# Batched q·kᵀ in float32: another order of the 32 KB chunks in the 4 MB loads

## The chip, the cores and the metric

The kernel runs on one core of one Trainium2 chip. The metric is the device time of one execution in microseconds. One execution was also taken with the hardware profiler, and all lines called "the profile" or "the trace" are from that one. The engines are called PE (matrix multiply), PEld (its weight loads), ACT, DVE and POOL (elementwise work) and SP (here it only issues transfers). SBUF is the on-chip memory of 128 partitions, PSUM is where PE writes, and sixteen DMA engines move data between SBUF and HBM.

## The reference

```python
def setup_inputs():
    batch, n_heads, seq, head_dim = 8, 12, 1024, 64
    # q, k: float32 [8, 12, 1024, 64], random, times 0.1

def reference(q, k):
    return np.einsum('bhid,bhjd->bhij', q, k).astype(np.float32)
```

That is 96 independent heads. Each multiplies a 1024 x 64 matrix by the transpose of another one, with no scaling and no softmax. The inputs are 50.3 MB, the output is 402.7 MB.

## The kernel before, in words

**Blocks of heads.** The 96 heads are taken in order in nine blocks of 2, 2, 4, 8, 16, 16, 16, 16 and 16 heads (numbers 0 to 8). `EARLY = 3` is the number of the 8-head block, so the 16-head blocks are those with `i > EARLY`: blocks 4 to 8. While a block is multiplied, the next one is loaded, cast and transposed.

**Loading (`Block.load`, line 171).** A 16-head block of q, and then one of k, is 16 x 1024 rows of 64 floats, 4 MB, contiguous in HBM. It goes into `x_sb`, 128 partitions of 32 KB, in one transfer: partition p takes the p-th chunk of 32 KB, that is 128 rows, so that a head lies in eight neighbouring partitions. `x_sb` holds one such load at a time, so a load waits until POOL has cast the one before. The ten loads of blocks 4 to 8 are issued from ACT's queue, q and k of a block in turn: one in block 2 (head 1), two in each of blocks 3 (heads 2 and 7), 4 (heads 4 and 10), 5 and 6 (heads 2 and 9), and the last, k of block 8, in block 7 (`LOADS` and the default beside it). So q of a block is loaded up to two blocks ahead and k in the block before. Blocks 0 to 3 are loaded from SP's and ACT's queues at the very start.

**Casting (`cast_quads`, line 220, POOL).** A load is cast to float16 in pieces called halves. Each piece is one of two parts (`part`) and one of two cuts (`c`) of the load, and is written by four POOL instructions of 32 partitions, which also rearrange the quadrants: afterwards a 32-partition quadrant holds 32 of the 64 columns of the head dimension for 32 chunks. Three buffers (`half_sb`) rotate.

**Transposing (`transpose_quads`, line 239, DVE).** One DVE instruction turns each 32 x 32 square of such a piece and writes into `qk_sb`. There the 64 values of the head dimension are in partitions, for half of the heads in partitions 0 to 63 and for the other half in 64 to 127, and the rows of a head are along the free axis. A piece has 128 x 2048 values. For a 16-head block there are eight pieces, four of q and four of k. In the output pattern the 32 chunks are the innermost dimension, with a step of R = 128 values of two bytes.

**Multiplying (`scores`, line 439, PE).** Head n of the block reads partitions `half * 64` onwards and column group g, with `half, g = divmod(n, N // 2)`: heads 0 to 7 from the lower partitions, 8 to 15 from the upper ones. A head takes eight weight loads and sixteen matmuls of 64 x 128 by 64 x 512. ACT copies each 128 x 2048 result from PSUM to one of three output buffers `o_sb` (line 297; in the first head DVE takes a part). The first matmul of a block waits for all eight transposes of that block (`self.ready`).

**Storing (line 310, SP).** Each head is stored in one transfer of 4 MB from its `o_sb`: partition p holds eight rows of the output, 32 KB. SP waits for the copies before it issues. ACT, in turn, waits for the store of three heads ago before it writes into that buffer.

**The tail (`scores_split`, lines 345 to 374).** The last head is stored in parts. One half of it goes out in an indirect transfer on POOL's queue, in which rows 16 to 19 and 48 to 51 (`APART = (16, 48)`) are left out. These rows are computed once more into a small buffer and stored by SP (line 433).

Of the kernel before, what the change touches and what calls it, by code (L numbers as in the profile page):

```python
# [9 lines left out]
P = 128  # L10
# [53 lines left out]
def kernel(  # L64
# [6 lines left out]
    nc = tc.nc  # L71
# [10 lines left out]
    PE_BLOCKS, EARLY = 2, 3  # L82
# [31 lines left out]
    class Ring:  # L114


        def __init__(self, bufs):
            self.bufs, self.n = bufs, 0
            self.busy = [[] for _ in bufs]
# [11 lines left out]
    n, at = S * D // P * 2, 8 * S // 2  # L131
# [15 lines left out]
    class Block:  # L147
        def __init__(self, i, first, N):
            self.i, self.first, self.N = i, first, N
            self.by_pe = i < PE_BLOCKS  # L150
            self.R = N * S // P
            self.elems = self.R * D
            self.cut = max(1, -(-self.R * 32 // CHUNK))
            self.raw = [None] * 2
            self.landed = [[] for _ in range(2)]
            self.rows = [None] * 2
            self.halves = {}
            self.qk = qk_sb[i % 2]
            self.ready = []
            self.over = []  # L160

        def load(self, x, eng, landing=None):
            events = []
            if self.raw[x] is None:
                at = x * self.elems if self.i == EARLY else 0
                self.raw[x] = x_sb[:, at : at + self.elems]
                landing = input_landing[x]
                events = list(input_busy)
            src = flat[x][self.first * S : (self.first + self.N) * S]
            eng.wait(events)  # L170
            dma = eng.eng.dma_start(
                out=self.raw[x], in_=src.rearrange("(p r) d -> p (r d)", p=P)
            )
            self.landed[x].append(landing.start(dma))

        def load_head(self, n, x, eng, landing):
# [54 lines left out]
        def transpose_quads(self, x, part, c, held=()):  # L231
            buf, cast, busy = self.halves.pop((x, part, c))
            n, m = self.N * S // 4, self.R // self.cut
            dst = self.qk[x][:, part * n : (part + 1) * n].rearrange(
                "c (i r) -> c r i", i=32
            )[:, c * m : (c + 1) * m]
            before = blocks[self.i - 2].over if self.i >= 2 else []
            done = dve.run(
                lambda: nc.vector.transpose(  # L239
                    out=dst, in_=buf.rearrange("p (r i) -> p r i", i=32)  # L240
                ),
                [cast, *held] + before,
            )
            busy.append(done)
            self.ready.append(done)
# [17 lines left out]
            self.ready.append(done)  # L263

        def scores(self, n, side, regions, w):
            half, g = divmod(n, self.N // 2)
            cs = slice(half * D, (half + 1) * D)
            qT = self.qk[0].rearrange("c (g m t) -> c g t m", t=NT, m=P)
            kT = self.qk[1].rearrange("c (g j) -> c g j", j=S)
            buf, out_free, out_busy = outs.next()  # L270
            written = {}
            for u in range(NT // w):
                ps, ps_free, ps_busy = regions.next()
                for tt in range(w):
                    stationary = qT[cs, g, w * u + tt]
                    done = pe.run(
                        lambda: load_weights(stationary, half * D),
                        self.ready if n == 0 and u == 0 else [],
                        signal=False,
                    )  # L280
                    for j in range(2):
                        at = tt * S + j * 512
                        done = pe.run(
                            lambda: multiply(
                                ps[:, at : at + 512],
                                stationary,
                                kT[cs, g, j * 512 : (j + 1) * 512],
                                half * D,
                            ),
                            ps_free,  # L290
                            signal=tt == w - 1 and j == 1,
                        )
                dst = buf[:, w * u : w * u + w].rearrange("p t j -> p (t j)")
                by_dve = w == 1 and u % 2
                copier = dve if by_dve else act
                copied = copier.run(
                    lambda: (nc.vector.tensor_copy if by_dve else nc.scalar.copy)(  # L297
                        out=dst, in_=ps[:, : w * S]
                    ),
                    out_free + [done],  # L300
                )
                written[copier] = copied
                ps_busy.append(copied)
                for do in side.get(u, []):
                    do()
            self.over = [done]
            sp.wait(written.values())
            if self.first + n == 0:
                sp.wait(blocks[EARLY].landed[0])
            dma = nc.sync.dma_start(  # L310
                out=of[self.first + n].rearrange("(p t) j -> p (t j)", p=P),
                in_=buf.rearrange("p t j -> p (t j)"),
            )
            out_busy.append(store_landing[id(buf)].start(dma))

        def scores_split(self, n, regions, w):
            half, g = divmod(n, self.N // 2)
            cs = slice(half * D, (half + 1) * D)
            qT = self.qk[0][cs, g * S : (g + 1) * S]
            kT = self.qk[1][cs, g * S : (g + 1) * S]  # L320
# [42 lines left out]
            for t in range(w):  # L363
                for c in range(2):
                    done = gps.run(
                        lambda: nc.gpsimd.tensor_copy(  # L366
                            out=packed[:, t, 0, :, c], in_=rows[:, t, :, c]
# [7 lines left out]
                    out=out.rearrange("b h (m t) j -> (b h m) (t j)", t=T),  # L375
                    out_offset=bass.IndirectOffsetOnAxis(ap=place_sb, axis=0),
                    in_=first,
# [9 lines left out]
            for c in range(4):  # L387
                row = 4 * APART[c // 2] + 8 * (c % 2)
                dst = head[row : row + 4 * w].rearrange("(e t) j -> e (t j)", t=w)
                self.store_part(sp, rest_landing, dst, rest[c:16:4])  # L390

            buf, out_free, _ = outs.next()
# [42 lines left out]
    def load_weights(stationary, at, to=0):  # L435
        return nc.tensor.ldweights(stationary, tile_position=(at, to))  # L436

    def multiply(dst, stationary, moving, at, to=0):
        return nc.tensor.add_instruction(  # L439
            mybir.InstMatmult(  # L440
                name=nc.get_next_instruction_name(),
                ins=[nc.tensor.lower_ap(moving), nc.tensor.lower_ap(stationary)],
                outs=[nc.tensor.lower_ap(dst)],
                start_tensor_calc=True,
                stop_tensor_calc=True,
                ldweights=False,
                tile_position=(at, to),
                tile_size=(D, stationary.shape[1]),
            )
        )  # L450
# [33 lines left out]
    for x in range(2):  # L484
# [7 lines left out]
                out=ident,  # L492
                in_=ident,
# [120 lines left out]
```

## Time and profile before

| | |
|---|---|
| median of 3 runs | 1060.29 us (1058.93 to 1060.81) |
| the profiled execution | 1059.37 us, of which its span 1057.6 us |
| granted clock of PE | 1.000 |
| HBM read, written | 50.33 MB, 402.78 MB |
| DMA, mean over the span | 429 GB/s |
| PE busy | 702.3 us (66%) |
| ACT busy | 695.4 us (66%) |
| DVE busy | 436.5 us (41%) |
| POOL busy | 357.8 us (34%) |

The span runs from the first to the last instruction. Busy shares are averages over the whole span; the profile also cuts the span into 40 slices of 26.4 us, where a digit is the busy share in tenths. For DMA that digit is the mean of the sixteen engines. Queue q1 is the one that SP issues on, q10 is ACT's, q0 is POOL's. In the list of groups an entry gives the line of the kernel, the engine, the operation, the tiles and shapes, the count, then the busy time and the mean of one in ns, then the idle time ahead of it and what ended most of that. In the list of transfers the last number is the median time from issue to landing. In the chain each line has the start, the length and the work.

### The profile page before, as it was taken

What the parts mean: (1) busy time and instruction counts of PE and PEld (TensorE: products, weight loads), DVE (VectorE), ACT (ScalarE), POOL (GpSimd) and SP (SyncE); (2) the same over time, 40 slices, a digit from 0 to 9 for tenths busy, and PEclk for the clock granted to TensorE, in tenths of its full rate; (3) what the DMA queues carried; (4) which work ended last, traced back from release to release, by engine and by line L of the source; (5) the groups of instructions that cost most, each with busy time, mean ns of one, the idle gap of its engine ahead of it and who ended that gap; (6) DMA issues with size and microseconds to landing.
All of it is one profiled execution on the core that took longest, in us unless ns stands there. A gap on an engine that the chain in (4) does not pass through costs nothing.

```text
span 1057.6 us, 3358 instructions
## 1 busy us (share of the span) xinstructions
PE 702.3 (66%) x1572; PEld 127.5 (12%) x802; DVE 436.5 (41%) x57; ACT 695.4 (66%) x385; POOL 357.8 (34%) x223
## 2 busy tenths in 40 slices
PE   6875744783756774765775675677477777777771
PEld 1111100110111110110111111111011111111110
DVE  2995929339254339137036706303930900000001
ACT  4766755674756765765875675577487777778771
POOL 7926455463708024605320830802290000000000
DMA  9999999999999999999999999999999999999998
GB/s 377 436 437 434 428 431 429 436 433 418 435 432 434 429 429 430 428 435 433 436 432 419 436 434 432 436 431 429 429 434 431 433 431 434 434 434 431 431 430 362
DMA packets 17185, 453.21 MB, mean 429 GB/s; under 512 B 1928, under 2 KB 1928, under 8 KB 2952
## 3 DMA queue, kind: packets, MB, share of 16 engines
q1 hardware_dynamic: 15008, 408.03, 89.6%
q10 hardware_dynamic: 2016, 42.99, 9.7%
q0 software_dynamic: 144, 1.97, 0.4%
q8 instruction: 9, 0.15, 0.0%
q14 instruction: 8, 0.07, 0.0%
HBM read 50.33 MB, written 402.78 MB: 428 GB/s over the span
## 4 chain that ended last, share of the span: by engine, by line
DMA 65%; ACT 15%; PE 8%; DVE 6%; POOL 4%; issue 1%; SPq 0%; ACTq 0%
DMA out_dram<-o_sb 60%; ACT o_sb L297 15%; PE ps_all L439 7%; DVE kT L239 4%; POOL half L220 3%; DMA x_sb<-in_k_dram 2%; DMA x_sb<-in_q_dram 2%; DVE qT L239 1%; DMA o_sb<-in_q_dram 0%; DVE x_sb L345 0%; DVE o_sb L345 0%; PE ps_all L253 0%; POOL qT L191 0%; DVE kT L260 0%; ACT kT L260 0%
## 5 line engine op out<-in xcount | busy, mean ns | idle before, releaser
L439 PE MATMUL ps_all<-kT,qT 64*128 64x512 f16 x1536 | 696.3, 617 | 325.5 <-ACT o_sb L297 307.7
L297 ACT COPY o_sb<-ps_all 128x2048 f32<-128x2048 f32 (+1 forms) x380 | 687.5, 1859 | 330.1 <-DMA out_dram<-o_sb 285.6
L220 POOL CAST half<-x_sb 32x2048 f16<-32x2048 f32 x176 | 332.1, 1887 | 431.3 <-DMA x_sb<-in_q_dram 176.2
L239 DVE STREAM_TRANSPOSE qT<-half 128x2048 f16<-128x2048 f16 x22 | 203.0, 9434 | 218.3 <-PE ps_all L439 117.8
L239 DVE STREAM_TRANSPOSE kT<-half 128x2048 f16<-128x2048 f16 x22 | 203.0, 9466 | 176.4 <-ACT o_sb L297 150.7
L436 PEld LDWEIGHTS <-qT 64*128 64x128 f16 x768 | 124.1, 162 | 894.5 <-issue 873.2
L345 DVE COPY x_sb<-ps_all 128x2048 f32<-128x2048 f32 x1 | 2.3, 2292 | 183.1 <-PE ps_all L439 183.1
L374 POOL DMA_INDIRECT out_dram<-x_sb,place x1 | 1.2, 1153 | 185.7 <-DVE x_sb L345 185.7
L366 POOL COPY rest_q<-qT 64x8 f16<-64x8 f16 x4 | 0.6, 196 | 51.1 <-DVE kT L239 51.1
L239 DVE STREAM_TRANSPOSE kT<-kT 128x1024 f16<-128x1024 f16 x2 | 9.4, 4893 | 0.0
L239 DVE STREAM_TRANSPOSE qT<-qT 128x1024 f16<-128x1024 f16 x2 | 9.2, 4786 | 0.0
L220 POOL CAST qT<-o_sb 32x1024 f16<-32x1024 f32 x8 | 8.3, 1034 | 1.2 <-DMA o_sb<-in_q_dram 0.8
L220 POOL CAST kT<-o_sb 32x1024 f16<-32x1024 f32 x8 | 8.3, 1034 | 0.5
L260 DVE COPY qT<-ps_all 128x1024 f16<-128x1024 f16 x2 | 2.4, 1224 | 11.2 <-PE ps_all L253 11.2
L297 DVE COPY o_sb<-ps_all 128x1024 f32<-128x1024 f32 x4 | 4.9, 1224 | 4.4 <-PE ps_all L439 4.4
L253 PE MATMUL ps_all<-ident,qT 128*128 128x128 f16 x16 | 2.1, 311 | 6.9 <-POOL qT L191 6.8
L345 ACT COPY x_sb<-ps_all 128x2048 f32<-128x2048 f32 (+1 forms) x2 | 3.7, 1860 | 2.1 <-PE ps_all L439 2.1
L260 ACT COPY kT<-ps_all 128x1024 f16<-128x1024 f16 x1 | 1.0, 1012 | 4.9 <-PE ps_all L253 4.9
L345 DVE COPY o_sb<-ps_all 128x2048 f32<-128x2048 f32 x1 | 2.3, 2291 | 3.7 <-PE ps_all L439 3.7
L191 POOL CAST qT<-o_sb 128x512 f16<-128x512 f32 x4 | 2.3, 613 | 3.9 <-DMA o_sb<-in_q_dram 3.9
L260 ACT ACT_TABLE_LOAD x1 | 1.3, 1283 | 2.8 <-issue 2.8
L260 DVE COPY kT<-ps_all 128x1024 f16<-128x1024 f16 x1 | 1.2, 1225 | 4.4 <-PE ps_all L253 4.4
(18 smaller groups left out, 14.5 us busy)
## 6 DMA issues: line engine op xcount, KB each, us to landing
out_dram<-o_sb SPq DMA_DIRECT2D x95, 4096.0 KB, 21.7
x_sb<-in_q_dram ACTq DMA_DIRECT2D x5, 4096.0 KB, 23.8
x_sb<-in_k_dram ACTq DMA_DIRECT2D x5, 4096.0 KB, 24.7
x_sb<-in_q_dram SPq DMA_DIRECT2D x1, 2048.0 KB, 14.6
x_sb<-in_k_dram SPq DMA_DIRECT2D x1, 2048.0 KB, 19.4
out_dram<-o_sb SPq DMA_DIRECT2D x1, 2048.0 KB, 17.9
o_sb<-in_k_dram ACTq DMA_DIRECT2D x4, 256.0 KB, 4.9
o_sb<-in_q_dram SPq DMA_DIRECT2D x4, 256.0 KB, 5.2
```

The source lines that it names most:

```text
L191: lambda: nc.gpsimd.tensor_copy(out=rows[:, :, h], in_=self.raw[x][:, h * n : (h + 1) * n].rearrange("p (r d) -> p r d", d=D),),
L220: lambda: nc.gpsimd.tensor_copy(out=dst[q0 : q0 + 32].rearrange("p (r d) -> p r d", d=32), in_=raw[32 * b : 32 * b + 32, c * m : (c + 1) * ...
L239: lambda: nc.vector.transpose(out=dst, in_=buf.rearrange("p (r i) -> p r i", i=32)),
L253: lambda: nc.tensor.transpose(t_ps[:, t], rows[:, t], ident),
L260: lambda: copy(out=dst, in_=t_ps.rearrange("c t m -> c m t")), [done]
L297: lambda: (nc.vector.tensor_copy if by_dve else nc.scalar.copy)(out=dst, in_=ps[:, : w * S]),
L345: lambda: (nc.vector.tensor_copy if copier is dve else nc.scalar.copy)(out=dst[:, t * S : (t + w) * S], in_=ps[:parts, : w * S]),
L366: lambda: nc.gpsimd.tensor_copy(out=packed[:, t, 0, :, c], in_=rows[:, t, :, c]),
L374: nc.gpsimd.indirect_dma_start(out=out.rearrange("b h (m t) j -> (b h m) (t j)", t=T), out_offset=bass.IndirectOffsetOnAxis(ap=place_sb, a ...
L436: return nc.tensor.ldweights(stationary, tile_position=(at, to))
L439: return nc.tensor.add_instruction(mybir.InstMatmult(name=nc.get_next_instruction_name(), ins=[nc.tensor.lower_ap(moving), nc.tensor.lower ...
```

## The change

In blocks 4 to 8, which the new flag `woven` marks, the chunk of a load that a partition takes is another one: partition 8e + j (e from 0 to 15, j from 0 to 7) takes chunk 16j + e, where it took chunk 8e + j. The source of the transfer has three dimensions for that, e, j and the 8192 floats of a chunk; the destination is written as before. Head n of the block has chunks 8n to 8n + 7. With the new order they are in partitions 8e + j with j = n // 2, and e from 0 to 7 for an even head or 8 to 15 for an odd one. After the casts, which are the same, the even heads are therefore in partitions 0 to 63 and the odd ones in 64 to 127, and each of the eight pieces holds a part of every head of a parity. The transposes write the 32 chunks in a four-dimensional pattern (rows, then e, then j innermost, with a step of 1024 values between neighbouring j), and a head reads `half, g = n % 2, n // 2`. The order in which heads are computed and stored, and the blocks 0 to 3, are the same.

```diff
@@ class Block, __init__
             self.by_pe = i < PE_BLOCKS
+            self.woven = i > EARLY
             self.R = N * S // P
...
+        def where(self, n):
+            return (n % 2, n // 2) if self.woven else divmod(n, self.N // 2)
+
         def load(self, x, eng, landing=None):
...
-            dma = eng.eng.dma_start(
-                out=self.raw[x], in_=src.rearrange("(p r) d -> p (r d)", p=P)
-            )
+            dst, src = self.raw[x], src.rearrange("(p r) d -> p (r d)", p=P)
+            if self.woven:
+                src = src.rearrange("(j e) f -> e j f", j=8)
+            dma = eng.eng.dma_start(out=dst, in_=src)
...
         def transpose_quads(self, x, part, c, held=()):
             buf, cast, busy = self.halves.pop((x, part, c))
             n, m = self.N * S // 4, self.R // self.cut
-            dst = self.qk[x][:, part * n : (part + 1) * n].rearrange(
-                "c (i r) -> c r i", i=32
-            )[:, c * m : (c + 1) * m]
+            src = buf.rearrange("p (r i) -> p r i", i=32)
+            if self.woven:
+                dst = self.qk[x].rearrange("c (j q e r) -> c q r e j", q=2, e=4, r=self.R)
+                dst = dst[:, part, c * m : (c + 1) * m]
+                src = src.rearrange("p r (e j) -> p r e j", e=4)
+            else:
+                dst = self.qk[x][:, part * n : (part + 1) * n].rearrange(
+                    "c (i r) -> c r i", i=32
+                )[:, c * m : (c + 1) * m]
...
-                lambda: nc.vector.transpose(
-                    out=dst, in_=buf.rearrange("p (r i) -> p r i", i=32)
-                ),
+                lambda: nc.vector.transpose(out=dst, in_=src),
...
         def scores(self, n, side, regions, w):
-            half, g = divmod(n, self.N // 2)
+            half, g = self.where(n)
...
         def scores_split(self, n, regions, w):
-            half, g = divmod(n, self.N // 2)
+            half, g = self.where(n)
```

## The prediction

> **What bounds the kernel now.** I read the rows of forty slices first, then the table of queues, then the chain that ended last, then the waits, and only then the groups of instructions.
>
> ```profile
> DMA  9999999999999999999999999999999999999998
> GB/s 377 436 437 434 428 431 429 436 433 418 435 432 434 429 429 430 428 435 433 436 432 419 436 434 432 436 431 429 429 434 431 433 431 434 434 434 431 431 430 362
> DMA packets 17185, 453.21 MB, mean 429 GB/s; under 512 B 1928, under 2 KB 1928, under 8 KB 2952
> ...
> q1 hardware_dynamic: 15008, 408.03, 89.6%
> q10 hardware_dynamic: 2016, 42.99, 9.7%
> ...
> DMA 65%; ACT 15%; PE 8%; DVE 6%; POOL 4%; issue 1%; SPq 0%; ACTq 0%
> ```
>
> The sixteen DMA engines are busy in every slice; no compute engine is above 66%. q1 is SP's queue (the stores), q10 is ACT's (the loads of the 16-head blocks). Two prices follow. Stores: 89.6% of 1057.6 us is 947.6 us on each engine for 408.03/16 = 25.50 MB, so 32 KB take 1.218 us. Loads: 9.7% is 102.6 us for 42.99/16 = 2.687 MB, so 32 KB take 1.251 us. The single packet records of the trace say where that difference sits: nearly all packets of 32 KB take 1.213 us, but in four of the five loads of k 22 to 30 of the 128 take longer, up to 2.33 us.
>
> ```profile
> PE ps_all L439 <- ACT o_sb L297: 307.7, 185, 11.6
> ACT o_sb L297 <- DMA out_dram<-o_sb: 285.6, 86, 11.6
> ```
> ```profile
> 151.19 36.71 DVE kT L239 x4
> 187.90 0.05 issue
> 187.94 1.94 PE ps_all L439 x4
> ...
> 197.38 21.36 DMA out_dram<-o_sb
> ```
>
> The first fence is from the list of waits (total us, times, longest): PE waits for ACT, and ACT for stores to free an output buffer, so the compute side runs ahead of the DMA. The second is the chain in order of time at the start of block 4, the tightest place: four transposes hold PE until 187.94, yet the store issued at 197.38 lands 21.36 us later. A store alone fills the engines for 9.7 us (8 packets of 1.218 us each), so 11.7 us of earlier work was still queued. Compute may be 11.7 us late there before the DMA runs dry; in the stretches with stores alone the same margin is 12.0 us (21.7 less 9.7). The time is therefore the DMA engines' work, the slowest engine's, plus a start and a tail. The execution took 1059.37 us, 1.8 more than its span, and 0.9 under the median of the runs, 1060.29.
>
> **The change part by part.** Bytes, loads, queues, issue points, head order and waits stay. Three things move.
>
> (1) The addresses on PE's side: head n reads half n%2, group n//2. Same shapes and counts, 1536 matmuls of 617 ns, and PE idles 325.5 us before them: nothing.
>
> (2) The writes of 40 of the 44 large transposes (eight for each of blocks 4 to 8).
>
> ```profile
> L239 DVE STREAM_TRANSPOSE kT<-half 128x2048 f16<-128x2048 f16 x22 | 203.0, 9466 | 176.4 <-ACT o_sb L297 150.7
> ...
> L239 DVE STREAM_TRANSPOSE kT<-kT 128x1024 f16<-128x1024 f16 x2 | 9.4, 4893 | 0.0
> ```
>
> Neighbouring results now lie 2048 bytes apart in runs of 8, where they lay 256 bytes apart. The rows hold three steps already: 64 bytes (block 2), 128 (block 3) and 256. They cost 4893/1024 = 4.78 and 9466/2048 = 4.62 ns a column, so the step does not set the price. I take zero. Against it: 2048 is eight times the widest step seen. The cover is the 11.7 us at block 4, so four transposes may each be 2.9 us (31%) slower at no cost; if they took twice as long, 37.9 - 11.7 = 26 us would be lost there. In later blocks they end over 30 us ahead of the block. A gain has no taker, since DVE sets nothing.
>
> (3) The loads themselves: ten of 4 MB, two for each of blocks 4 to 8.
>
> ```profile
> x_sb<-in_q_dram ACTq DMA_DIRECT2D x5, 4096.0 KB, 23.8
> x_sb<-in_k_dram ACTq DMA_DIRECT2D x5, 4096.0 KB, 24.7
> ```
>
> Issue: the source has three dimensions now. ACT's load issues take 0.334 us; the oddly shaped stores of line 433 took up to 1.286 us on SP. Ten times 0.95 us on ACT, with the next copies to o_sb behind it, lies under the 11.7 us: nothing.
>
> Transfer: each load lands in sixteen parts, one for each engine. Before, source and destination both begin with a dimension of 128. Now the source begins with 16 (e), with 8 inside (j), while the destination keeps 128. I expect the split to follow the 16, so that engine e takes partitions 8e to 8e+7 in turn. The old grouping must be another one: the tail of this kernel keeps rows 16 to 19 and 48 to 51 out of its indirect store together, which is the share of one engine if an engine has four partitions and the four that lie 32 higher. A side of SBUF laid out for that grouping is then entered by two engines at once: e and e+4 are both in partitions that are 32 apart.
>
> What that costs no row shows. The bounds: below, the loads lose their whole excess over the stores, 80 packets on an engine (10 loads, 8 each) by 1.251 - 1.218, which is -2.6 us. Above, two engines share what one had throughout, and every load packet takes twice as long: 80 x 1.218 = +97 us. The nearest rows are the disturbed packets: 2.33 us at worst, 1.9 times the normal one, so a doubling is what a meeting of two streams costs here. How often they would meet is also in the records: the engines run in step. The sixteen landings of the first load of block 4 lie within 0.67 us; later loads spread to 1.3 to 2.4 us, but most of their landings keep within 0.9. Two engines that start a load packet some 0.17 us apart, which is close to the nearest pairs, overlap for all but that. As a store lands with its slowest engine and the next one needs its buffer, the nearest pair sets the pace: 80 x (1.218 - 0.17) = +84 us. A pair that shares fairly keeps its distance, so this would not fade.
>
> The Trainium skill has both halves of this. "DMA: Bandwidth & Descriptors", in "Why a DMA increments its semaphore by 16 and not by 1" and "The descriptor swizzle", says that the number of engines comes from the slowest dimension of each side and that a 128-partition transfer is dealt out in fours with the fours 32 higher. "SBUF — State Buffer", in "Door 1: The DMA port swizzle", gives sixteen ports of about 27 GB/s and puts partitions 32 apart on the same one; by it the woven loads would use eight ports at a time, at half the rate, an estimate of +97 us. The trace agrees as far as 27 GB/s for an engine (32 KB in 1.213 us); no run here shows the ports.
>
> Sum: 1059.4 + 84 + 0 + 0 = 1143.4 us for an execution like the profiled one; with the 0.9 us to the median, 1144. The later landing of the loads adds nothing on top: at each block start the queued stores are late by as much as the transposes.
>
> **The rivals.** About 0.2%, 2.1 us, is what a measurement of this kernel can tell from no change.
>
> *The pairs fall out of step.* The same sharing, but one of two engines is served first and the other falls a packet behind; from then on one loads while the other stores. Lost: between one packet for each load, 10 x 1.2 = 12 us, and half of the full sum, 42 us. For it: phases in the later loads do spread to over 1 us. Against it: in the stretches with stores alone the distances between the sixteen landings of a store hold for hundreds of us. About 1080 us.
>
> *Faster: the reading order.* All sixteen engines read neighbouring chunks, 512 KB in one piece at a time, instead of pieces spread over 4 MB. If the slow packets of k's loads are a matter of which places in HBM are read beside the stores, and nothing is lost in SBUF, the excess of 2.6 us goes: 1057.7 us. It decides only from four fifths of that excess up (2.1 us), and the loads of q, dealt out the same way, have almost no slow packets, which speaks against the order as their cause.
>
> *Nothing.* The change may not do what I read into it: if the split follows the destination's 128, every engine keeps its partitions and only the places read change. Part of the excess comes or goes: 1058.5 to 1062, about 1060.
>
> *The transposes pay for the wider step.* 26 us at block 4 if they double, 1086 us. The even price at three steps speaks against it.
>
> **How the numbers follow.** Loads slowed in step 0.55, 1115 to 1158 us; out of step 0.14, 1063 to 1110; transposes 0.04; nothing 0.15; faster 0.12 (of "nothing" I count all as within 0.2%). Slower is 0.55 + 0.14 + 0.04 = 0.73. As 0.27 lie at or under no change, a range with 8 in 10 has to reach down to them: 1057.5 to 1157. The likeliest case's own range is 1115 to 1158.
>
> **What would show it.** Right: q10's time on an engine grows from 102.6 us to about 187, so some 16% of a span near 1142; loads land after 31 to 34 us instead of 24; the slices with a load fall towards 300 GB/s while DMA stays at 9; the stores alone after 860 us keep 9.75 us a head; L239 keeps 9.4 us. Wrong: q10 stays under 10% and the landings at 24 us (nothing, or faster); q10 grows in the first loads only (out of step); L239 at 12 us or more, with DMA below 9 near the start of block 4 (transposes).

## The result, and the profile after

The changed kernel takes 1120.97 us (median of 6 runs, 1115.75 to 1123.96) against 1060.17 us (6 runs, 1058.93 to 1060.81). The ratio is 1.0569, with a 95% interval of 1.0541 to 1.0597: 60.8 us slower. The profiled execution has a span of 1115.8 us, 58.2 more than before.

The same parts of the page as before, in the same order: the slices, the queues, the shares of the chain, the large transposes, and the loads with their time to landing.

```profile
DMA  9999999999999999999999999999999999999997
GB/s 375 432 375 410 395 375 416 385 432 331 433 394 403 435 430 325 432 435 345 431 432 395 359 432 398 366 429 435 382 407 435 431 437 432 435 431 433 432 431 325
...
q1 hardware_dynamic: 15008, 408.03, 85.8%
q10 hardware_dynamic: 2016, 42.99, 13.3%
...
DMA 67%; ACT 15%; PE 7%; DVE 5%; POOL 3%; issue 1%; SPq 0%; ACTq 0%
...
L250 DVE STREAM_TRANSPOSE kT<-half 128x2048 f16<-128x2048 f16 x22 | 202.7, 9433 | 205.6 <-ACT o_sb L306 148.3
...
x_sb<-in_q_dram ACTq DMA_DIRECT2D x5, 4096.0 KB, 30.1
x_sb<-in_k_dram ACTq DMA_DIRECT2D x5, 4096.0 KB, 31.3
```

The DMA engines are still busy in every slice, and they move the same bytes more slowly. That is the trap of a busy row: a packet that takes longer counts as busy for all of its time. The GB/s row tells where. Apart from the first slice and the last, those without a load stay at 429 to 437, and those with one fall to 325 to 416. The two queues say how much: q10 takes 13.3% of 1115.8 us, 148.4 us on each engine, where it took 102.6; q1 takes 85.8%, 957.4 us, where it took 947.6. Together that is 45.8 + 9.8 = 55.6 of the 58.2 us. A load's 32 KB went from 1.25 to 1.81 us, and the stores lost a fifth as much in all, although nothing about them was changed.

Windows of the traces show the first of the ten loads, with store packets between its own, and then a stretch with stores alone: first in the changed kernel, then in the kernel before. The columns after the length are the busy times of the compute engines (PE, PEld, DVE, ACT, POOL), the granted clock, the share of the DMA and its rate.

```profile
67.20:92.40 25.20, 11.74 (x27) 2.10 (x13) 15.72 (x2) 11.39 (x7) 0.00 (x0) 1.00 1.00 336
...
870.00:1040.00 170.00, 126.71 (x281) 22.25 (x140) 27.54 (x3) 126.83 (x71) 0.58 (x4) 1.00 1.00 433
```
```profile
67.80:85.30 17.50, 9.27 (x22) 1.61 (x10) 15.50 (x2) 9.30 (x6) 0.00 (x0) 1.00 1.03 446
...
870.00:1030.00 160.00, 119.85 (x265) 21.26 (x132) 0.40 (x1) 119.72 (x66) 0.00 (x0) 1.00 1.00 433
```

While the first load runs, the rate is 336 GB/s at a busy share of 1.00; before it was 446 at 1.03 (a packet counts where it starts, so a short window can come out a little high). With stores alone it is 433 in both. The waits of the compute side follow from this:

```profile
PE ps_all L448 <- ACT o_sb L306: 364.3, 185, 17.9
ACT o_sb L306 <- DMA out_dram<-o_sb: 342.7, 87, 17.9
```

ACT waits 57 us longer for stores than before. That is the whole loss seen from the other end, not a second one.

### The profile page after: what moved, and what is told of

Same layout as the page of the kernel before. It is cut to its first block, busy times and chain, and to the rows that moved or that the text cites. A ratio compares the mean times of both kernels' runs of the same rounds, so it can differ in the third digit from the quotient of the medians.

```text
span 1115.8 us, 3358 instructions
## 1 busy us (share of the span) xinstructions
PE 702.3 (63%) x1572; PEld 126.1 (11%) x802; DVE 436.1 (39%) x57; ACT 695.3 (62%) x385; POOL 357.8 (32%) x223
## 3 DMA queue, kind: packets, MB, share of 16 engines
q1 hardware_dynamic: 15008, 408.03, 85.8%
q10 hardware_dynamic: 2016, 42.99, 13.3%
q0 software_dynamic: 144, 1.97, 0.4%
## 4 chain that ended last, share of the span: by engine, by line
DMA 67%; ACT 15%; PE 7%; DVE 5%; POOL 3%; issue 1%; SPq 0%; ACTq 0%
DMA out_dram<-o_sb 61%; ACT o_sb L306 15%; PE ps_all L448 7%; DVE kT L250 4%; POOL half L225 3%; DMA x_sb<-in_k_dram 3%; DMA x_sb<-in_q_dram 3%; DVE qT L250 1%; DMA o_sb<-in_q_dram 0%; DVE x_sb L354 0%; DVE o_sb L354 0%; PE ps_all L262 0%; POOL qT L196 0%; DVE kT L269 0%; ACT kT L269 0%
## 6 DMA issues: line engine op xcount, KB each, us to landing
x_sb<-in_q_dram ACTq DMA_DIRECT2D x5, 4096.0 KB, 30.1
x_sb<-in_k_dram ACTq DMA_DIRECT2D x5, 4096.0 KB, 31.3
```

## The experiments

The theory: a first dimension of 16 in the source makes the transfer give engine e the partitions 8e to 8e+7, so that engines e and e+4 write into partitions 32 apart at the same time, and those share one way in. The rivals: the order of reading in HBM; the three-dimensional source as such; the layout that follows (the transposes' step, the alternating heads).

**Sixteen, in the old order.** Only the shape of the source is changed; the weave, the transposes' pattern and the alternating heads are left out.

```diff
 # kernel before, Block.load
-            dma = eng.eng.dma_start(
-                out=self.raw[x], in_=src.rearrange("(p r) d -> p (r d)", p=P)
-            )
+            src = src.rearrange("(p r) d -> p (r d)", p=P)
+            if self.i > EARLY:
+                c = self.elems
+                src = bass.AP(src.tensor, src.offset, [[8 * c - D, 16], [c, 8], [1, c]])
+            dma = eng.eng.dma_start(out=self.raw[x], in_=src)
```

> The kernel before, with one edit: the source of the ten 4 MB loads has a first dimension of 16 and 8 chunks inside, as in the changed kernel, but in the old order, partition 8e+j taking chunk 8e+j. So that the two dimensions do not melt into one, the step of e is shorter by one row of 64 floats: partition 8e+j reads its chunk from e rows earlier (at most 15 of its 128 rows), so heads of blocks 4 to 8 get slightly wrong rows. Layout, transposes and heads are those of before. Sharing theory (the first dimension of 16 gives engine e partitions 8e to 8e+7, and engines e and e+4 then write into partitions 32 apart in step): as slow as the changed kernel, 1112 to 1128 us, load packets near 1.8 us, the ACT queue near 13% of the engines' time. Reading order (sixteen neighbouring chunks at once are what is slow): no slower than 1065 us. Layout theory (the transposes' 2 KB step or the alternating heads): 1060 us.

Measured: 1121.21 us, ratio 1.0569 (1.0551 to 1.0586), the changed kernel's own. Queues and loads of its profile:

```profile
q1 hardware_dynamic: 15008, 408.03, 85.6%
q10 hardware_dynamic: 2016, 42.99, 13.5%
...
x_sb<-in_q_dram ACTq DMA_DIRECT2D x5, 4096.0 KB, 30.6
x_sb<-in_k_dram ACTq DMA_DIRECT2D x5, 4096.0 KB, 30.9
```

So neither the weave, nor neighbouring reads, nor the layout is needed for the loss. The shape of the source alone makes it.

**First dimension 32.** The weave stays, in a shape that begins with 32.

```diff
 # changed kernel
-            return (n % 2, n // 2) if self.woven else divmod(n, self.N // 2)
+            return (n % 4 // 2, n // 4 * 2 + n % 2) if self.woven else divmod(n, self.N // 2)
...
-                src = src.rearrange("(j e) f -> e j f", j=8)
+                src = src.rearrange("(j e) f -> e j f", j=4)
...
-                dst = self.qk[x].rearrange("c (j q e r) -> c q r e j", q=2, e=4, r=self.R)
+                dst = self.qk[x].rearrange("c (j q e r) -> c q r e j", q=2, e=8, r=self.R)
...
-                src = src.rearrange("p r (e j) -> p r e j", e=4)
+                src = src.rearrange("p r (e j) -> p r e j", e=8)
```

> The changed kernel with its weave in another shape, and the reference's output: the source has a first dimension of 32 with 4 inside, partition 4g+i takes chunk 32i+g. Neighbouring chunks are still read at the same time, the source still has three dimensions, the transposes still write with a wide step (4 KB instead of 2 KB), heads still alternate between the halves (two and two). Only the split over the engines may differ: 32 goes over 128 in fours, so that each engine can keep the partitions it had before. Sharing theory: the loss is gone, 1057 to 1063 us, loads land after 24 us, packets of 1.21 us. Reading order or the three-dimensional source or the layout as cause: 1100 us or more. If the neighbouring order also removes the slow packets in the loads of k, up to 2.6 us less than before: 1057.5 us.

Measured: 1060.36 us, ratio 1.0003 (0.9993 to 1.0013). Queues, transposes and loads:

```profile
q10 hardware_dynamic: 2016, 42.99, 9.7%
...
L250 DVE STREAM_TRANSPOSE kT<-half 128x2048 f16<-128x2048 f16 x22 | 202.8, 9449 | 174.6 <-ACT o_sb L306 147.1
...
x_sb<-in_q_dram ACTq DMA_DIRECT2D x5, 4096.0 KB, 25.0
x_sb<-in_k_dram ACTq DMA_DIRECT2D x5, 4096.0 KB, 25.3
```

The loss is gone with the three dimensions, the interleaved reads and an even wider step in the transposes all in place. One number of the source decides, 16 against 32; the other edited lines only follow it. The hope for 2.6 us from the reading order is not borne out either: q10 stays at 9.7%, and single packets above 1.23 us, up to 2.5 us, are still there, now in loads of q as well.

**Forms alone.** Transfers by themselves, four in flight, in one execution. The loops are shortened here; after each of them the kernel waits for all its transfers.

```diff
+    for m in range(8): load_plain(m)      # 128 chunks in order
+    for m in range(8): load_sixteen(m)    # "(j e) f -> e j f", j=8
+    for m in range(8): load_fours(m)      # "(j e) f -> e j f", j=4
+    for m in range(8): load_low(m)        # partitions 0 to 63, in order
+    for m in range(8): store_plain(m)
+    for m in range(8): store_sixteen(m)
```

> No product at all, only transfers, each form by itself and four in flight: eight loads of 4 MB in order, eight with the changed kernel's source (first dimension 16), eight with first dimension 32, eight of 2 MB into partitions 0 to 63, eight stores of 4 MB in order, eight stores whose destination has the first dimension 16. Sharing theory: loads in order 1.21 us for 32 KB, 9.7 us for each load; first dimension 16 twice that when nothing else is in the queue, 2.43 us and 19.4 us; first dimension 32 as in order, 9.7 us; partitions 0 to 63 alone also at half rate, 9.7 us for 2 MB. Stores with first dimension 16 slowed too, if reading is shared as writing is. Reading order: first dimensions 16 and 32 equally slow, partitions 0 to 63 at full rate (4.9 us for 2 MB).

One window for each form, in that order; the last column is the rate:

```profile
2.00:81.10 79.10, 0.00 (x0) 1.00 0.99 423
83.00:243.00 160.00, 0.00 (x0) 1.00 1.00 209
245.20:324.00 78.80, 0.00 (x0) 1.00 0.99 424
325.80:407.90 82.10, 0.00 (x0) 1.00 1.00 204
409.80:487.80 78.00, 0.00 (x0) 1.00 1.00 428
489.50:617.00 127.50, 0.00 (x0) 1.00 0.92 263
```

Loads with sixteen run at 209 GB/s, half of 423; with 32 at 424; 64 partitions in plain order at 204. Stores with sixteen are slowed as well, but not evenly; as no store with a first dimension of 32 was run, the order in which they write to HBM is not ruled out as their cause. In the GB/s row of the page they begin at 303 near the end, and the rate climbs:

```profile
GB/s 373 434 424 430 434 225 223 203 203 203 216 225 203 203 203 193 417 441 441 428 386 203 203 203 203 203 305 417 430 441 441 303 218 235 256 282 299 337 345 97
```

The loads of sixteen stay at 203 to 225 to their end; the stores start at 218 and reach 345, and 97 belongs to the last slice, of which the engines are busy only two tenths.

**Two halves.** Nothing of the change, only two plain transfers for each load.

```diff
 # kernel before, Block.load
-            dma = eng.eng.dma_start(
-                out=self.raw[x], in_=src.rearrange("(p r) d -> p (r d)", p=P)
-            )
-            self.landed[x].append(landing.start(dma))
+            src = src.rearrange("(p r) d -> p (r d)", p=P)
+            parts = [slice(0, 64), slice(64, P)] if self.i > EARLY else [slice(0, P)]
+            for s in parts:
+                dma = eng.eng.dma_start(out=self.raw[x][s], in_=src[s])
+                self.landed[x].append(landing.start(dma))
```

> The kernel before, with the reference's output and one edit: each of the ten 4 MB loads is two transfers, partitions 0 to 63 and then 64 to 127, each with a plain two-dimensional source in the old order. Nothing of the change is in it. Sharing theory: sixteen engines inside 64 partitions meet two by two just as in the changed kernel, so it is as slow: 1110 to 1130 us. Reading order, three-dimensional source or layout as cause: as before, 1059 to 1063 us, ten more issues of 0.33 us on ACT being covered.

Measured: 1117.23 us, ratio 1.054 (1.0522 to 1.0559). Its queue:

```profile
q10 hardware_dynamic: 2176, 42.99, 13.2%
```

Nearly the same loss from a kernel that, by the theory, shares only one thing with the change: sixteen engines at work in partitions that meet in twos.

**Two by columns**, the control for that: the parts are `[:, :h]` and `[:, h:]` of all 128 partitions.

> The control for the loads in two halves: the kernel before, each of the ten 4 MB loads as two transfers again, but of all 128 partitions and half of the columns each (16 KB a packet). The reference's output. Sharing theory: 1059 to 1063 us, since every engine keeps its own partitions; a second transfer costs nothing. If the splitting itself (twice as many transfers in ACT's queue) was the cause: 1110 to 1130 us, as with the halves.

Measured: 1066.65 us, ratio 1.0064 (1.0047 to 1.008), outside of what I had expected. The loads' queue of its profile:

```profile
q10 hardware_dynamic: 3456, 42.99, 9.7%
```

The loads themselves are not slowed. A second transfer for each load is not free; where those 6 us go was not pursued. But it is a ninth of the loss of the halves.

**Which partitions share.** Loads in order into parts of the partitions, again in one execution and shortened; eight plain stores follow.

```diff
+    for lo, hi in ((0, 128), (0, 64), (0, 32), (32, 64), (0, 16)):
+        for m in range(8): load(m, lo, hi)      # 32 KB for each partition
```

> No product, only loads in order of 32 KB for each partition, eight of a kind with four in flight: into partitions 0 to 127, 0 to 63, 0 to 31, 32 to 63 and 0 to 15; then eight stores of 4 MB. If partitions 32 apart share one way in, partitions 0 to 31 take 1 MB in half the time that 0 to 63 take for 2 MB, at the same 203 GB/s, and 32 to 63 the same: the 32 partitions more bring nothing. Partitions 0 to 15 then have half of those ways, about 100 GB/s. If each partition or each engine had its own limit instead, 0 to 31 would run at half the rate of 0 to 63, about 100 GB/s, and 0 to 15 at a quarter.

The windows, in that order, the stores last:

```profile
2.00:80.80 78.80, 0.00 (x0) 1.00 1.00 425
82.70:164.70 82.00, 0.00 (x0) 1.00 0.99 204
166.50:207.90 41.40, 0.00 (x0) 1.00 0.98 202
209.60:251.00 41.40, 0.00 (x0) 1.00 0.98 203
252.80:290.90 38.10, 0.00 (x0) 1.00 0.99 110
293.10:371.20 78.10, 0.00 (x0) 1.00 1.00 430
```

Partitions 0 to 31 take 202 GB/s, 32 to 63 take 203, and 0 to 63 together 204: 32 partitions more bring nothing, so the two sets of 32 share their way in. Sixteen partitions take 110, about half, so the way is shared in parts finer than a set. Which partition has which partner these windows do not show; partners 32 apart fit them. The Trainium skill, "SBUF — State Buffer", "Door 1: The DMA port swizzle", says of its sixteen ports that partitions 32 apart are on the same one, with 196 GB/s for 64 partitions at 1 MiB; the trace agrees as far as the sets go.

**How much of the sharing is lost beside stores.** The changed kernel and the kernel before, each with `next_load(act)` made `next_load(sp)`.

> The changed kernel, its ten loads issued on SP's queue, behind the stores, and not on ACT's. On each DMA engine the eight packets of a load then run in a row, where they alternated with packets of stores. Alternation theory (a load packet that waits for its neighbour's overlaps with the store packets between, so only 0.72 us of the full 1.3 us is lost for each): all sixteen engines now load at the same time with nothing between, each load packet takes the 2.5 us of the forms run alone, and the loss is 10 x 8 x 1.3 = 104 us beyond that of the same kernel with loads in order: about 1165 us. Rival (a load packet of this form costs its 0.72 us wherever it runs): 1115 to 1125 us.

> The control for that: the kernel before, its ten loads on SP's queue. Both theories: the same bytes at the same rate, 1057 to 1063 us, as long as loads that queue behind two stores (landing after about 31 us instead of 24) do not come too late for block 4, which has 11.7 us of margin; if they do, up to 10 us more.

Measured: 1148.74 us, ratio 1.0843 (1.0825 to 1.0861), for sixteen; 1062.79 us, ratio 1.0024 (1.0015 to 1.0034), for the loads in order. Loads of the two:

```profile
x_sb<-in_q_dram SPq DMA_DIRECT2D x5, 4096.0 KB, 39.0
x_sb<-in_k_dram SPq DMA_DIRECT2D x5, 4096.0 KB, 38.6
```
```profile
x_sb<-in_q_dram SPq DMA_DIRECT2D x5, 4096.0 KB, 31.3
x_sb<-in_k_dram SPq DMA_DIRECT2D x5, 4096.0 KB, 31.2
```

With a load's packets in a row, the loss is 86.0 us, 1.07 us for each of the 80 load packets of an engine; alternating with stores it was 60.8 us, 0.76 us each. Alone, by 209 and 423 GB/s, 32 KB take 2.51 and 1.24 us, so 1.27 us is the full price. The direction is as the alternation theory had it and its rival is out, but 104 us was too much. That engines enter a load some us apart, so that at its two ends some load while others still store, would account for the rest. The packet records fit this: in each of the first four loads the packets above 1.5 us lie within 21 us and take 2.39 to 2.44 us on average; in each of the last four they are spread over 29 to 32 us and take 2.17 to 2.24. It was not tried by itself.

**Only the loads of q.** The first experiment with `and x == 0` added to its condition.

> The kernel before, with the source of first dimension 16 (old order, the step of e one row short, so q's rows in blocks 4 to 8 are slightly shifted and the product is off there) for the five loads of q alone; k's are as before. Sharing theory: a loss for each load, so half of it: 1060 + 5 x 6.0 = about 1090 us, q's landings near 30 us and k's near 25 us. If the loss came once (engines knocked out of step for the rest of the run): near 1120 us, with k's loads slow too.

Measured: 1087.43 us, ratio 1.0252 (1.0235 to 1.0269).

```profile
x_sb<-in_q_dram ACTq DMA_DIRECT2D x5, 4096.0 KB, 31.1
x_sb<-in_k_dram ACTq DMA_DIRECT2D x5, 4096.0 KB, 23.4
```

Five loads cost 27.1 us, 5.4 each; the ten of the change cost 6.1 each. The price goes by the load and leaves nothing behind: k's loads land sooner than before (23.4 against 24.7 us).

## Why the prediction was right, and where it was off

**What bounds the kernel, and that the loss would come through the DMA:** right. DMA stays at 9 while the rate falls in the slices with loads, and the stretch with stores alone keeps 433 GB/s.

**The split follows the first dimension of 16:** the step on which all the rest hung, held at 0.55 plus 0.14. Sixteen in the old order (slow), 32 in a woven order (not slow) and plain halves (slow) show from three sides that the first dimension decides and that the collision is one of partitions. Which engine writes which partition is not in the trace; it is inferred from which shapes collide.

**The upper bound, twice the packet:** right by itself. Alone, the packet goes from 1.24 to 2.51 us. I had taken the doubling from the disturbed packets of k's loads, as a meeting of two streams; what disturbs those was not found, and in so far the right factor was luck.

**The term of 84 us:** mis-sized; it was 60.8. The step that failed is "two engines that start a load packet some 0.17 us apart". I had read the distance of two engines from the landings of a load that nothing disturbed; those of the other nine loads before spread over 1.3 to 2.7 us, and in the changed kernel those of each load spread over 2.6 to 3.5 us. The starts are no closer. By the packet records of the first woven load, four engines begin within 0.15 us, and their first load packets take 1.21 to 1.27 us, while the other twelve start 0.75 to 1.11 us after the first and take 1.69 to 1.98. And I had counted the store packet between as out of the matter. A load packet beside which on average fewer than 8 of the other 15 engines were at a load packet took 1.54 us, one with 10 or more 1.97; in the kernel before both kinds took 1.24. That reads as if engines that store at the time leave the others room. The stores lose too: in the windows of the loads store packets take 1.36 us in the middle instead of 1.21. On average the price of a load packet was 0.76 us and not 1.05. Which engine meets which is not in the trace, so how the discount comes about is a reading of these records.

**The out-of-step rival** may have a part in this, as engines that are not in step meet less often. It does not take the loss away: the load packets of the last round of a load are as long (1.77 us on average) as those of the first (1.77), and its sign, a q10 that grows in the first loads only, is missing, with a mean packet of 1.62 to 1.96 us in all ten loads and no fall towards the last. Only for the sixteen-wise stores alone does the rate climb, from 218 to 345 GB/s; that engines fall out of step there is a reading of the climb, not shown.

**Costs put at nothing:** the transposes took 9.43 us at a step of 2 KB and 9.43 to 9.45 at 4 KB (9.43 to 9.47 before); the matmuls took 618 ns (617 before); the issues took 0.54 us instead of 0.33, as they did in the 32-wise form, which lost nothing. The later landings added nothing on top at block 4, as forecast: its first store is issued at 210.36 and lands 26.11 us later, so 16.4 us of work were still queued:

```profile
200.92 1.94 PE ps_all L448 x4
...
210.36 26.11 DMA out_dram<-o_sb
```

**The signs I named:** q10 was to reach 187 us and 16%, and reached 148.4 and 13.3%, by the same term. Landings of 31 to 34 us: 30.1 and 31.3, just under and just in. The slices with a load were to fall towards 300 GB/s and fell to 325 to 416. The time lies within the likeliest case's own range (1115 to 1158), near its lower end. The full range, 1057.5 to 1157, reached down to no change, so that it held says little.

**The faster rival** fell: the neighbouring order in the 32-wise form brought no gain that can be told from none.

## What to carry to other kernels

A rearranged source can leave packets, bytes and their size alone and still change which engine writes which partitions; where DMA is the bound, look at the first dimension of both sides before the order of reading. If a weave is wanted, let its first dimension be 32 where the destination has 128: here that cost nothing that can be told from none (1.0003), and 16 cost 5.7%. When transfers collide, price the collision from a run of the form alone, and expect a discount where its packets alternate with others; here 0.76 us of 1.27 were left.

## What the runs showed of the hardware that I had not expected

Plain transfers of 64 neighbouring partitions, in the middle of other traffic, cost nearly as much as the change: 1.054 against 1.0569. The Trainium skill, "DMA: Bandwidth & Descriptors", "Rules for kernel authors", asks for an outermost dimension that is a multiple of 16 to use all engines; the trace has all sixteen engines busy (a DMA share of 1.00), and loads still ran at 209 GB/s alone, so that rule is not enough for the full rate. Stores in the sixteen-wise form are slowed too (263 GB/s against 428), from a cause that was not separated. And the slow packets in k's loads are not a matter of the reading order: they stay with the neighbouring order of the 32-wise form, and in the run where only q's loads were sixteen-wise, every packet of k's took 1.213 to 1.225 us, in an unchanged order.
